# A hybrid attention, recurrence and mixture-of-experts layer: expert weights in 8 KB rows, the overfull path ahead of the first expert pair, and p turned inside the recurrence

## The chip, the core and the metric

One Trainium2 chip, one of its cores. The metric is device time in microseconds of one execution. Kernel before: median 1132.77 us of 3 runs (1131.93 to 1135.42).

## The reference, cut to what matters

One layer over 512 tokens of width 1024, all float32.

```python
h = rmsnorm(x, g_mix)
q, k, v, xr, gr, ga, gb = split(h @ w_in)
A = diff_attention(q, k, v) @ w_attn_br
R = (rg_lru(conv4(xr)) * gelu(gr)) @ w_lru_br
x += (sigmoid(ga) * A + sigmoid(gb) * R) @ w_out
t = rmsnorm(x, g_moe)
# top-1 of 4 groups, top-2 of its 8 experts: 32 experts, FF 512
for e in range(32):
    x += c[e] * ((silu(t @ w_e_gate[e]) * (t @ w_e_up[e])) @ w_e_down[e])
x += sigmoid(rmsnorm(x, g_ple) @ w_ple_gate) * (p @ w_ple_proj)
out = rmsnorm(x, g_final)
```

## The kernel before, in words

Tokens stand in four tiles `t` of 128 rows. Dense weights come as 1 MB pieces `wr`; ScalarE rounds each into `wh` (L157) and VectorE or GpSimd takes the rest `wl` (L160); TensorE then does three matmuls per block (wh with the high and the low half of the input, wl with the high half). `wh` and `wl` have three buffers each.

**The recurrence (to about 193 us).** For each of eight blocks `m` TensorE does xr, the gates, gr and merge (L169 to L171, L354 to L356). `lru_back` runs for two blocks at a time, one pair late: a square root on ScalarE, products on GpSimd (L384), scans `hs` and products on VectorE (L386, L387), `yh` on ScalarE (L389), `yl` on GpSimd. After the last merge TensorE turns `p` (`pT_ps`, eight transposes, L426), ScalarE and VectorE split it in two halves (`pth` L428, `ptl` L429), and 48 matmuls (`pp_ps`, L438 to L440) give p @ w_ple_proj, which goes to DRAM (L443) for the end of the kernel. The R projection follows.

**The experts (598 to 1067 us).** Experts go in 16 pairs. Each takes 12 pieces of 1 MB (gate, up, down, four each; L825), issued by the SyncE queue into a ring of 15 buffers; a piece has 4 KB rows and carries both experts of the pair. `pair_front` (L994) does gate and up, `hidden_t` turns the hidden block (L978), `pair_back` (L1008) does down. `gather` (L700) picks the tokens of two pairs by one-hot matmuls out of `hx`, the normalised rows that `split_tokens` (L683, L684) writes; since a piece holds rows 2p and 2p+1 in partition p, the gather reads `hx` with a stride of 2. `scatter_two` and `comb` (L959 to L970) add the outputs. In `in_order` blocks TensorE keeps the order of the program.

**The overfull path.** An expert has 64 slots. `count` writes `nblk_i`, the number of extra rounds; `tc.If(nb > 0)` (L1135) runs `overflow`, a loop over all experts. It stands between hidden_t of pair 15 and that pair's down block. The data here never take it: `nb` is 0, every engine loads the value and branches past the body.

**The tail (1067 us on).** The weights of the last gate are loaded (`gate_load`, L800), split, and multiplied for four token tiles.

Of the kernel before, what the change touches and what calls it, by code (L numbers as in the profile page):

```python
# [19 lines left out]
P = 128  # L20
D = 1024
# [19 lines left out]
def kernel(  # L41
# [35 lines left out]
    ONCE = 2  # L77

# [36 lines left out]
    gmv = T("gmv")[:4, :256]  # L115
# [98 lines left out]
    nc.sync.dma_start(gmv, g_moe.rearrange("o (h c) -> (o h) c", h=4))  # L214
# [84 lines left out]
    for k in range(2):  # L299
        nc.tensor.transpose(pv[:, 1 + k, 0:4], gmv[:, k:k + 255:2], ident[:4, :4])  # L300
    gm2 = const.tile([P, 8], F32, name="gm2")
    nc.vector.tensor_copy(gm2.rearrange("p (h k) -> p k h", k=2), pv[:, 1:3, 0:4])
# [89 lines left out]

    TB, TA = {}, {}
# [8 lines left out]
    for j in range(4):  # L402
# [19 lines left out]
    pth, ptl = ([lx.tile([P, S], F32R, tag="lx", bufs=4, name=n) for _ in range(2)] for n in ("pth", "ptl"))
    for k in range(2):
        pt = tps("pT_ps")
        for t in range(NT):
            nc.tensor.transpose(pt[:, t, :], pl[t // 2][:, t % 2 * PLE + k * P:t % 2 * PLE + (k + 1) * P], ident)  # L426
        pt = pt.rearrange("p a b -> p (a b)")
        nc.scalar.activation(pth[k], pt, AF.Copy)  # L428
        nc.vector.tensor_sub(ptl[k], pt, f32(pth[k]))  # L429
# [14 lines left out]
    lx_stack.close()  # L444
# [233 lines left out]
    def split_tokens(t, hx):  # L678

        HX[t] = hx  # L680
        for i in range(2):
            cs = slice(i * 512, (i + 1) * 512)
            nc.scalar.activation(hx[:, 0, cs], xm[:, t, cs], AF.Copy, scale=rstd2[:, t:t + 1])  # L683
            nc.vector.scalar_tensor_tensor(hx[:, 1, cs], xm[:, t, cs], rstd2[:, t:t + 1], f32(hx[:, 0, cs]),  # L684
                                           op0=ALU.mult, op1=ALU.subtract)
# [125 lines left out]
    def loads():  # L811
        for pr, nm, src in pair_order():
            for h in range(4):
                n = P if nm == "d" else 2 * P
# [85 lines left out]
    def gather(q):  # L900
# [7 lines left out]
        for k in range(0, KT, 2):  # L908
# [74 lines left out]
    def pair_front(pr, xg, fill):  # L983
# [20 lines left out]
    def pair_back(pr, hT, fill=None):  # L1004
        py = [zps("y_ps") for _ in range(2)]
        for f, i in [(f, i) for f in range(4) for i in range(2)]:
            for e in range(2):
                nc.tensor.matmul(py[i][64 * e:64 * e + 64, :], hT[:, f, 64 * e:64 * e + 64],  # L1008
                                 W[pr, "d", f][0][:, e, i * 512:(i + 1) * 512], start=f == 0, stop=f == 3)
# [5 lines left out]
    def overflow(nb):  # L1015

        scratch = [t.rearrange("p e (k f) -> p (e k) f", k=2) for t in spill]
# [5 lines left out]
        with tc.For_i(0, nb):  # L1023
            with tc.For_i(0, NE) as e:
# [79 lines left out]
    def experts(pr):  # L1104
# [9 lines left out]
        if pr < 15:  # L1114
            expert_outputs(pr)
# [164 lines left out]
```

## Time and profile before

| | |
|---|---|
| median of 3 runs | 1132.77 us |
| the profiled execution, its time | 1134.24 us |
| its span on the core | 1132.5 us |
| TensorE busy | 1090.8 us, 96% |
| VectorE, ScalarE, GpSimd busy | 565.5, 380.4, 155.6 us |
| DMA rate in the expert stage | 409 GB/s |
| mean granted TensorE clock | 0.987 |

Durations below are of the profiled execution; start times are microseconds from the start of its span. "Idle before" names what ended a wait. [...]

### The profile page before, as it was taken

The page shows a single profiled execution, that of the slowest core. Times are in us where ns is not written, and L with a number is a line of the kernel's source. Part 1 is how long each engine was busy: PE and PEld are TensorE (multiplying, and loading weights), DVE is VectorE, ACT ScalarE, POOL GpSimd, SP SyncE. Part 2 cuts the span into 40 slices and gives each one's busy share as a digit, 9 for nine tenths or more (in the row PEclk, how much of TensorE's full clock was granted, in tenths as well). Part 3 has the DMA queues.
Part 4 walks back from the last instruction along what each step waited for, and adds up shares of the span by engine and source line. Part 5 has one row for each costly group of instructions (what it writes and reads, how often), then busy time and mean ns, then how long its engine had stood idle before and what let it go on. Part 6 is the DMA issues. An engine that isn't in the chain of part 4 may idle for free. (4 is left out here: it accounts for less than half of the span.)

```text
span 1132.5 us, 14421 instructions
## 1 busy us (share of the span) xinstructions
PE 1090.8 (96%) x5650; PEld 732.4 (65%) x5650; DVE 565.5 (50%) x1080; ACT 380.4 (34%) x770; POOL 155.6 (14%) x142
## 2 busy tenths in 40 slices
PE   8999996999999999999999999999999999999897
PEld 7777775888788878778984535454535353533376
DVE  6766673325657474764474343433433433232574
ACT  5556554125545463633431202020201111100353
POOL 3242323111212021332100000000000000000021
PEclk9999998999999999999999999999999999999899
DMA  7332143322221312235857999999999999999801
GB/s 207 112 112 75 58 147 110 100 93 75 76 75 38 100 51 75 75 80 203 317 186 259 408 409 408 409 409 409 409 409 409 408 409 409 409 408 407 341 26 56
DMA packets 109794, 259.81 MB, mean 229 GB/s; under 512 B 12477, under 2 KB 56090, under 8 KB 109722
## 3 DMA queue, kind: packets, MB, share of 16 engines
q1 hardware_dynamic: 109722, 258.84, 60.5%
q8 instruction: 46, 0.75, 0.3%
q14 instruction: 26, 0.21, 0.1%
HBM read 254.63 MB, written 4.19 MB: 229 GB/s over the span
## 5 line engine op out<-in xcount | busy, mean ns | idle before, releaser
L157 ACT ACTIVATE wh<-wr 128x1024 fp32r<-128x1024 f32 x81 | 85.6, 1058 | 105.9 <-PE R_ps L170 32.4
L1008 PE MATMUL y_ps<-d,hT 128*64 128x512 f32 x512 | 117.1, 608 | 4.2 <-PEq L1135 3.6
L994 PE MATMUL gu_ps<-g,xg 128*64 128x512 f32 x512 | 116.0, 595 | 0.6 <-DMA g<-in_w_e_gate_dram 0.6
L994 PE MATMUL gu_ps<-u,xg 128*64 128x512 f32 x496 | 110.1, 593 | 1.4 <-DMA u<-in_w_e_up_dram 0.6
L160 DVE TENSOR_TENSOR wl<-wr,wh 128x1024 fp32r<-128x1024 f32 x54 | 73.0, 1352 | 61.5 <-ACT wh L157 60.2
L160 POOL TENSOR_TENSOR wl<-wr,wh 128x1024 fp32r<-128x1024 f32 x27 | 64.9, 2404 | 181.3 <-ACT wh L157 167.8
L999 ACT ACTIVATE sg<-gu_ps 128x512 f32<-128x512 f32 x16 | 9.6, 598 | 232.4 <-PE gu_ps L994 232.4
L1008 PEld LDWEIGHTS y_ps<-d,hT 128*64 128x64 f32 x512 | 35.9, 139 | 74.1 <-issue 68.5
L994 PEld LDWEIGHTS gu_ps<-u,xg 128*64 128x64 f32 x496 | 35.2, 137 | 72.8 <-issue 66.4
L994 PEld LDWEIGHTS gu_ps<-g,xg 128*64 128x64 f32 x512 | 35.2, 137 | 70.8 <-issue 64.6
L1000 DVE TENSOR_TENSOR sg<-sg,gu_ps 128x512 f32<-128x512 f32 x16 | 11.0, 687 | 126.1 <-ACT sg L999 126.1
L202 POOL TENSOR_TENSOR s<-msq,mhalf 128x1 f32<-128x1 f32 x4 | 3.7, 915 | 499.5 <-DVE msq L201 499.5
L971 DVE TENSOR_TENSOR xm<-xm,comb_ps 128x1024 f32<-128x1024 f32 x30 | 36.6, 1221 | 65.5 <-PE comb_ps L970 65.5
L700 PE MATMUL xg_ps<-oneh,wr 128*128 128x256 f32 x384 | 58.3, 291 | 2.1 <-DVE oneh L692 2.1
L953 DVE SCALAR_TENSOR_TENSOR yl<-y_ps,c,yh 128x512 fp32r<-128x512 f32 x30 | 22.5, 750 | 72.9 <-ACT yh L952 71.4
L700 PEld LDWEIGHTS xg_ps<-oneh,wr 128*128 128x128 f32 x384 | 52.7, 201 | 2.7 <-DVE oneh L692 2.2
L952 ACT ACTIVATE yh<-y_ps,c 128x512 fp32r<-128x512 f32 x30 | 20.6, 688 | 100.2 <-PE y_ps L1008 100.2
L171 PE MATMUL merge_ps<-hTh,wl 128*128 128x512 f32 x128 | 51.9, 406 | 0.5 <-POOL wl L160 0.5
L169 PE MATMUL merge_ps<-hTh,wh 128*128 128x512 f32 x128 | 51.5, 402 | 0.0
L170 PE MATMUL merge_ps<-hTl,wh 128*128 128x512 f32 x128 | 51.4, 401 | 0.0
L962 DVE TENSOR_TENSOR xm<-xm,comb_ps 128x512 f32<-128x512 f32 x68 | 43.6, 679 | 2.6 <-PE comb_ps L960 2.6
L921 ACT ACTIVATE xg<-xg_ps,gm 128x256 f32<-128x256 f32 x60 | 25.2, 470 | 49.2 <-PE xg_ps L700 48.8
(328 smaller groups left out, 2512.9 us busy)
## 6 DMA issues: line engine op xcount, KB each, us to landing
g<-in_w_e_gate_dram SPq DMA_DIRECT2D x64, 1024.0 KB, 19.3
d<-in_w_e_down_dram SPq DMA_DIRECT2D x64, 1024.0 KB, 19.8
u<-in_w_e_up_dram SPq DMA_DIRECT2D x62, 1024.0 KB, 20.2
wr<-in_w_in_dram SPq DMA_DIRECT2D x26, 1024.0 KB, 5.1
wr<-in_w_lru_br_dram SPq DMA_DIRECT2D x4, 1024.0 KB
wr<-in_w_attn_br_dram SPq DMA_DIRECT2D x4, 1024.0 KB, 5.3
wr<-in_w_out_dram SPq DMA_DIRECT2D x4, 1024.0 KB, 5.1
wr<-in_w_ple_gate_dram SPq DMA_DIRECT2D x3, 1024.0 KB
```

The source lines that it names most:

```text
L157: nc.scalar.activation(hi, src, AF.Copy)
L160: e.tensor_sub(lo, src, f32(hi))
L169: nc.tensor.matmul(out_ps, wh[:, k, :], th(k), start=k == 0, stop=False)
L170: nc.tensor.matmul(out_ps, wh[:, k, :], tl(k), start=False, stop=False)
L171: last = nc.tensor.matmul(out_ps, wl[:, k, :], th(k), start=False, stop=k == KT - 1)
L700: nc.tensor.matmul(o, HX[t][:, i, c0:c0 + 255:2], oneh[:, t, :], start=t == 0 and i == 0 and k % 2 == 0, stop=t == NT - 1 and i == 1 and k ...
L921: nc.scalar.activation(xg[(k + c) // 2][:, (k + c) % 2, :], pt[:, c, :], AF.Copy, scale=gm2[:, k + c:k + c + 1])
L953: nc.vector.scalar_tensor_tensor(yl, y, c[:, 0:1], f32(yh), op0=ALU.mult, op1=ALU.subtract)
L962: nc.vector.tensor_tensor(xs_, xs_, pc, op=ALU.add)
L971: nc.vector.tensor_tensor(xm[:, t, :], xm[:, t, :], pc.rearrange("p a b -> p (a b)"), op=ALU.add)
L994: last = nc.tensor.matmul(gu[i][64 * e:64 * e + 64, :], xg[k // 2][:, k % 2, o + 64 * e:o + 64 * e + 64], W[pr, nm, k // 2][0][:, e, k % 2 ...
L1008: nc.tensor.matmul(py[i][64 * e:64 * e + 64, :], hT[:, f, 64 * e:64 * e + 64], W[pr, "d", f][0][:, e, i * 512:(i + 1) * 512], start=f == 0 ...
```

## The change

Five parts, on six places of the code (line numbers below are those of before; those of the changed kernel are up to 11 higher, so L157 is L158 there, L994 is L1004, L1135 is L1142).

1. **8 KB pieces.** A piece of weights now holds half of one expert: four rows of gate or up (two of down) per partition, 8 KB in a row. It is still 1 MB. Pieces 0 and 1 of a weight are the first halves of the two experts, so both are needed at the start of a block, and 2 and 3 at its middle.
2. **Rows in the gather's order.** `split_tokens` reads the token row with a stride of four elements and writes it so that the gather reads 128 contiguous columns; `hidden_t` reads with a stride of 2 instead.
3. **The overfull path** moves from the end of the experts to right behind `gather(0)`. It uses the four buffers of pair 0's gate weights as scratch and loads them again.
4. **gate_load(0)** is issued ahead of the last pair's down pieces.
5. **p is turned** in one two-bank PSUM tile ahead of block 7, its halves take a `wh` and a `wl` buffer, and the pp sums of two token tiles share a two-bank tile.

```diff
+    def turn_p():
+        pth = wp.tile([P, 2, S], F32R, tag="wh", bufs=3, name="pth")
+        ptl = wp.tile([P, 2, S], F32R, tag="wl", bufs=3, name="ptl")
+        pt = sps("pT_ps")
+        for k in range(2):
+            for t in range(NT):
+                nc.tensor.transpose(pt[:, k, t * P:(t + 1) * P],
+                                    pl[t // 2][:, t % 2 * PLE + k * P:t % 2 * PLE + (k + 1) * P], ident)
+        nc.scalar.activation(pth, pt, AF.Copy)
+        nc.vector.tensor_sub(ptl, pt, f32(pth))
...
         for m in (2 * j, 2 * j + 1):
+            if m == 7:
+                pth, ptl = turn_p()
             lru_front(m, wx, wg, m % 2)
...
-            pz = zps("pp_ps")
+            if t % 2 == 0:
+                pz2 = sps("pp_ps")
+            pz = pz2[:, t % 2, :]
...
-            nc.scalar.activation(hx[:, 0, cs], xm[:, t, cs], AF.Copy, scale=rstd2[:, t:t + 1])
+            src = xm[:, t, i * 512:(i + 1) * 512].rearrange("q (p k) -> q k p", k=4)
+            hi, lo = (hx[:, n, i * 512:(i + 1) * 512].rearrange("q (k p) -> q k p", k=4) for n in range(2))
+            nc.scalar.activation(hi, src, AF.Copy, scale=rstd2[:, t:t + 1])
...
-                c0 = k // 2 * 256 + k % 2
-                nc.tensor.matmul(o, HX[t][:, i, c0:c0 + 255:2], oneh[:, t, :],
+                nc.tensor.matmul(o, HX[t][:, i, k * P:(k + 1) * P], oneh[:, t, :],
...
+            if pr == 15 and nm == "d":
+                for b in range(W_EARLY):
+                    gate_load(b)
...
-                s_ = src[0, 2 * pr:2 * pr + 2, h * n:(h + 1) * n, :]
+                n, k = (256, 2) if nm == "d" else (512, 4)
+                s_ = src[0, 2 * pr + h % 2, h // 2 * n:(h // 2 + 1) * n, :].rearrange("(p k) f -> p (k f)", k=k)
...
-            nc.tensor.transpose(pt[:, f, :], sg[:, f * P:(f + 1) * P], ident)
+            c0 = f // 2 * 256 + f % 2
+            nc.tensor.transpose(pt[:, f, :], sg[:, c0:c0 + 255:2], ident)
...
+    xg = gather(0)
+    nb = nc.values_load(nblk_i[0:1, 0:1], min_val=0, max_val=4)
+    with tc.If(nb > 0):
+        overflow(nb)
+    load_upto(NRING + ONCE)
     with in_order():
-        xg = gather(0)
-        load_upto(NRING + ONCE)
         SG[0] = pair_front(0, xg, front_fill(0))
         for pr in range(NE // 2):
             experts(pr)
-    spill = [RING("spill") for _ in range(4)]
-    nb = nc.values_load(nblk_i[0:1, 0:1], min_val=0, max_val=4)
-    with tc.If(nb > 0):
-        overflow(nb)
-    with in_order():
-        expert_outputs(15)
```

How the instructions move, at three places. First ScalarE around the merge of block 6 (`mg_1239` before, `mg_1241` now). Before, in the order of the queue (`wh_1242` and `wh_1296` are the xr and gr weights of block 7, `wh_1331` those of merge 7):

```order
L157 ACTIVATE wh_1242<-wr_1098 128x1024 [waits PE_49]
L349 ACTIVATE xch_1138<-xc_1133 128x512 [waits DVE_49]
L157 ACTIVATE wh_1296<-wr_1100 128x1024 [waits PE_49]
L359 ACTIVATE t_r_1149<-gate_ps_1142,hb_297 128x512 [waits PE_49]
L360 ACTIVATE t_i_1150<-gate_ps_1142,hb_297 128x512 [waits Activation_49]
L363 ACTIVATE lru_103<-t_r_1149,hn_301 128x512 [waits Activation_49]
L372 ACTIVATE sq_1187<-gr_ps_1158 128x512
L364 ACTIVATE t_r_1149<-t_r_1149,hn_301 128x512 [waits Activation_49]
L389 ACTIVATE yh_1198<-lru_106 128x512 [waits DVE_49]
L375 ACTIVATE sq_1187<-sq_1187 128x512 [waits DVE_49]
L157 ACTIVATE wh_1331<-wr_1102 128x1024 [waits PE_49,Pool_49]
L389 ACTIVATE yh_1206<-lru_106 128x512 [waits DVE_49]
```

Now (`wh_1257` and `wh_1311` are the xr and gr weights of block 7, `wh_1346` those of merge 7):

```order
L365 ACTIVATE t_r_1151<-t_r_1151,hn_303 128x512 [waits Activation_49]
L390 ACTIVATE yh_1200<-lru_106 128x512 [waits DVE_49]
L376 ACTIVATE sq_1189<-sq_1189 128x512 [waits DVE_49]
L390 ACTIVATE yh_1208<-lru_106 128x512 [waits DVE_49]
L414 ACTIVATE mg_1241<-merge_ps_1212 128x512 [waits PE_49]
L403 ACTIVATE pth_1243<-pT_ps_1245 128x1024 [waits PE_49]
L158 ACTIVATE wh_1257<-wr_1100 128x1024
L158 ACTIVATE wh_1311<-wr_1102 128x1024 [waits Pool_49]
L158 ACTIVATE wh_1346<-wr_1104 128x1024 [waits DVE_49,PE_49]
```

The weights of block 7 were rounded ahead of the second `yh`; now they stand behind it, behind the merge's own activation and behind `pth`.

Second VectorE at the end of the recurrence, with the second half of w_ple_proj (`wl_1444` before, `wl_1440` now). Before:

```order
L160 TENSOR_TENSOR wl_1444<-wr_1397,wh_1443 128x1024 [waits PE_49,Activation_49]
L365 SCALAR_TENSOR_TENSOR lru_104<-t_i_1287,xc_1270 128x512 [waits Activation_49]
L373 TENSOR_SCALAR sq_1324<-sq_1324 128x512 [waits Activation_49]
L374 TENSOR_TENSOR sq_1324<-sq_1324,gr_ps_1295 128x512 [waits DVE_49]
L367 SCALAR_TENSOR_TENSOR lru_105<-lru_105,t_r_1286 128x512 [waits Activation_49,Pool_49]
L376 SCALAR_TENSOR_TENSOR lru_106<-sq_1324,gr_ps_1295 128x512 [waits Activation_49]
L386 SCALAR_TENSOR_TENSOR hs_1363<-lru_103,lru_105 128x512 [waits Pool_49]
L386 SCALAR_TENSOR_TENSOR hs_1371<-lru_103,lru_105 128x512 [waits Pool_49]
L387 SCALAR_TENSOR_TENSOR lru_106<-hs_1363,lru_106 128x512 [waits DVE_49]
L387 SCALAR_TENSOR_TENSOR lru_106<-hs_1371,lru_106 128x512 [waits DVE_49]
L429 TENSOR_TENSOR ptl_1381<-pT_ps_1383,pth_1379 128x512 [waits Activation_49]
```

Now:

```order
L368 SCALAR_TENSOR_TENSOR lru_105<-lru_105,t_r_1301 128x512 [waits Activation_49,Pool_49]
L161 TENSOR_TENSOR wl_1398<-wr_1395,wh_1397 128x1024 [waits DMAHW4_49,PE_49,Activation_49]
L377 SCALAR_TENSOR_TENSOR lru_106<-sq_1339,gr_ps_1310 128x512 [waits Activation_49]
L387 SCALAR_TENSOR_TENSOR hs_1378<-lru_103,lru_105 128x512 [waits DMAHW2_49,Pool_49]
L387 SCALAR_TENSOR_TENSOR hs_1386<-lru_103,lru_105 128x512 [waits DMAHW3_49,Pool_49]
L388 SCALAR_TENSOR_TENSOR lru_106<-hs_1378,lru_106 128x512 [waits DVE_49]
L388 SCALAR_TENSOR_TENSOR lru_106<-hs_1386,lru_106 128x512 [waits DVE_49]
L161 TENSOR_TENSOR wl_1440<-wr_1395,wh_1439 128x1024 [waits PE_49,Activation_49]
```

`ptl` has left this place; the low half of the second weight has come behind the two scans.

Third TensorE where the branch stands. Before, ahead of the last pair's down block:

```order
L978 MATMUL hT_ps<-ident,sg 128x128 [waits DVE_49]
L978 MATMUL hT_ps<-ident,sg 128x128 x3
L1134 TENSOR_LOAD nblk_i [waits DVE_49,PE_49,Pool_49]
L1135 COMPARE_AND_BRANCH
L1023 COMPARE_AND_BRANCH
```

Now, behind the last matmuls of gather(0):

```order
L709 MATMUL xg_ps<-oneh,hx_5229 128x256 [waits Activation_49]
L709 MATMUL xg_ps<-oneh,hx_5229 128x256 x7
L1141 TENSOR_LOAD nblk_i [waits DVE_49,PE_49,Pool_49]
L1142 COMPARE_AND_BRANCH
L1034 COMPARE_AND_BRANCH
```

The load and the branch have moved from the last of the 16 pairs to ahead of the first; what follows the second row in each is the start of the skipped body, and the other four engines' branches move along.

## Rows read from the trace of the kernel before

**Rows 1.** windows: stretch, length, busy by engine, granted clock, DMA share, GB/s.

```profile
650.00:1000.00 350.00, 350.00 (x1774) 165.79 (x1773) 130.83 (x205) 50.73 (x96) 0.00 (x0) 1.00 1.03 409
1000.00:1050.00 50.00, 47.38 (x212) 17.75 (x211) 15.39 (x21) 4.88 (x8) 0.00 (x0) 1.00 1.01 402
```

**Rows 2.** waits of PE, 138 to 195 us: total, times, longest.

```profile
PE pp_ps L440 <- DVE ptl L429: 5.0, 1, 5.0
PE pp_ps L438 <- ACT pth L428: 3.2, 1, 3.2
PE gate_ps L354 <- ACT xch L349: 0.7, 1, 0.7
```

**Rows 3.** windows of the stretches at half the clock; columns as in Rows 1.

```profile
175.30:185.60 10.30, 4.97 (x11) 3.48 (x12) 5.62 (x5) 2.72 (x5) 4.61 (x3) 0.50 0.04 15
588.30:591.80 3.50, 3.48 (x20) 3.38 (x21) 3.19 (x16) 0.21 (x1) 0.00 (x0) 0.51 0.99 401
1052.60:1059.40 6.80, 5.73 (x14) 1.94 (x16) 0.70 (x2) 0.00 (x0) 0.00 (x0) 0.50 0.77 292
```

**Rows 4.** timeline, 149 to 160 us: start, duration, instruction, [idle before <-releaser].

```profile
150.62 0.39 PE L169 MATMUL xr_ps<-hTh,wh 128*128 128x512 f32 x1
...
153.47 2.71 DVE L387 SCALAR_TENSOR_TENSOR lru<-hs,lru 128x512 f32<-128x512 f32 x1
...
156.21 0.64 ACT L389 ACTIVATE yh<-lru 128x512 fp32r<-128x512 f32 x1 [3.08 <-DVE lru L387]
...
157.22 1.05 ACT L157 ACTIVATE wh<-wr 128x1024 fp32r<-128x1024 f32 x1
...
158.30 1.23 DVE L160 TENSOR_TENSOR wl<-wr,wh 128x1024 fp32r<-128x1024 f32 x1 [0.81 <-ACT wh L157]
```

**Rows 5.** timeline, 168 to 190 us, PE and DVE.

```profile
169.83 1.03 PE L426 MATMUL pT_ps<-ident,pl 128*128 128x128 f32 x8
...
172.98 5.48 DVE L386 TENSOR_TENSOR_SCAN hs<-lru 128x512 f32<-128x512 f32 x2 [3.02 <-POOL lru L384]
...
178.39 1.26 DVE L387 SCALAR_TENSOR_TENSOR lru<-hs,lru 128x512 f32<-128x512 f32 x2
```

**Rows 6.** DMA, 620 to 1000 us: queue, packets, MB, share of 16 engines.

```profile
q1 hardware_dynamic: 40229, 155.08, 102.3%
```

**Rows 7.** DMA, 811.5 to 812.0 us: one 8 KB instruction packet in that stretch.

```profile
q14 instruction: 1, 0.01, 3.9%
```

**Rows 8.** timeline of PE, pairs 12 and 13 (first two) and 14 and 15.

```profile
970.49 7.08 PE L994 MATMUL gu_ps<-u,xg 128*64 128x512 f32 x32
...
987.61 7.09 PE L1008 MATMUL y_ps<-d,hT 128*64 128x512 f32 x32
...
1029.92 3.93 PE L994 MATMUL gu_ps<-u,xg 128*64 128x512 f32 x16
...
1037.04 1.94 PE L994 MATMUL gu_ps<-u,xg 128*64 128x512 f32 x8 [0.62 <-SPq L1135]
...
1041.34 5.58 PE L1008 MATMUL y_ps<-d,hT 128*64 128x512 f32 x24
...
1047.55 1.94 PE L1008 MATMUL y_ps<-d,hT 128*64 128x512 f32 x8 [0.62 <-SPq L1135]
```

**Rows 9.** line 1135, and waits of SP, 1000 to 1070 us.

```profile
L1135 PEldq COMPARE_BRANCH  x1: 4932/4932/4932, 1048.3 to 1048.3; - x1
...
SPq L1135 <- SPq L1135: 17.9, 8, 2.9
```

**Rows 10.** timeline, 1046 to 1060 us: ACT, then PE.

```profile
1050.12 0.59 ACT L980 ACTIVATE hT<-hT_ps 128x512 f32<-128x512 f32 x1
...
1053.67 6.47 PE L1008 MATMUL y_ps<-d,hT 128*64 128x512 f32 x16 [3.59 <-PEq L1135]
```

**Rows 11.** timeline, 583 to 599 us: DVE, then PE.

```profile
587.12 0.75 DVE L684 SCALAR_TENSOR_TENSOR hx<-xm,rstd,hx 128x512 fp32r<-128x512 f32 x1 [0.93 <-ACT hx L683]
...
588.32 2.29 PE L700 MATMUL xg_ps<-oneh,wr 128*128 128x256 f32 x9 [2.14 <-DVE oneh L692]
```

More of the change, by code (lines that the diff above doesn't have):

```diff
@@ L77 @@
     ONCE = 2
+    W_EARLY = 1
     def SM(name, shape, dt=F32, bufs=4):
@@ L298 @@
     nc.vector.tensor_copy(colv, pv[:, 0, :NV])
[L299 to L302, printed above, removed]
+    for k in range(4):
+        nc.tensor.transpose(pv[:, 1, 2 * k:2 * k + 2], gmv[:, k:k + 509:4], ident[:2, :2])
+    gm4 = const.tile([P, 8], F32, name="gm4")
+    nc.vector.tensor_copy(gm4.rearrange("p (h k) -> p k h", k=4), pv[:, 1, 0:8].rearrange("p (k h) -> p k h", h=2))
     hb = const.tile([P, 16], F32, name="hb")
@@ L391, in lru_back @@
             Y[m] = (yh, yl)
+    def turn_p():
[8 more added lines that the diff above has]
+        nc.vector.tensor_sub(ptl, pt, f32(pth))
+        return [pth[:, k, :] for k in range(2)], [ptl[:, k, :] for k in range(2)]
     TB, TA = {}, {}
@@ L418 @@
     lru_back((6, 7))
+    lx_stack.close()
     pp_dram = dram.tile([S, D], F32, name="pp_dram")
[L422 to L429, printed above, removed]
     wpp = WR([P, 2, D])
@@ L1008, in pair_back @@
                 nc.tensor.matmul(py[i][64 * e:64 * e + 64, :], hT[:, f, 64 * e:64 * e + 64],
-                                 W[pr, "d", f][0][:, e, i * 512:(i + 1) * 512], start=f == 0, stop=f == 3)
+                                 W[pr, "d", f // 2 * 2 + e][0][:, f % 2 * D + i * 512:f % 2 * D + (i + 1) * 512], start=f == 0, stop=f == 3)
             if fill:
@@ L1015, in overflow @@
     def overflow(nb):
-        scratch = [t.rearrange("p e (k f) -> p (e k) f", k=2) for t in spill]
+        late_routing()
+        scratch = [W[0, "g", h][0].rearrange("p (k f) -> p k f", k=4) for h in range(4)]
         V = lambda n: scratch[n // 4][:, n % 4, :]
@@ L1033, in overflow @@
                 for b in range(2):
+                    px = zps("xs2_ps")
+                    for t in range(NT):
+                        for i in range(2):
+                            nc.tensor.matmul(px, oneh[:, t, :], f32(HX[t][:, i, b * 512:(b + 1) * 512]),
+                                             start=t == 0 and i == 0, stop=t == NT - 1 and i == 1)
+                    nc.scalar.activation(V(13 + b).rearrange("s (p k) -> s k p", k=4), px.rearrange("s (k p) -> s k p", k=4), AF.Copy)
                     pt = tps("xg2_ps")
                     for c in range(4):
+                        nc.tensor.transpose(pt[:, c, :], V(13 + b)[:, c * P:(c + 1) * P], ident)
+                    for c in range(4):
                         k = 4 * b + c
-                        for t in range(NT):
-                            for i in range(2):
-                                nc.tensor.matmul(pt[:, c, :], f32(HX[t][:, i, k * P:(k + 1) * P]), oneh[:, t, :],
-                                                 start=t == 0 and i == 0, stop=t == NT - 1 and i == 1)
                         nc.scalar.activation(xg[b][:, c, :], pt[:, c, :], AF.Identity, scale=colv[:, C_GM + k:C_GM + k + 1])
@@ L1081, in overflow @@
             nc.vector.tensor_scalar(base, base, float(P - 1024 * NE), None, op0=ALU.add)
+        for h in range(4):
+            nc.sync.dma_start(*W[0, "g", h])
     C, SG, HT, PY, YW = {}, {}, {}, {}, {}
@@ L1132 @@
             experts(pr)
-    spill = [RING("spill") for _ in range(4)]
-    nb = nc.values_load(nblk_i[0:1, 0:1], min_val=0, max_val=4)
-    with tc.If(nb > 0):
-        overflow(nb)
-    with in_order():
-        expert_outputs(15)
-    for b in range(4):
+    for b in range(W_EARLY, 4):
         gate_load(b)
```

24 lines of the change are left out of this document (7 added, 17 removed).

## The prediction, made before the changed kernel was run

> **What bounds the kernel now.** Read the busy times first: TensorE is at 96% of the span, no other engine above 50%. So a microsecond counts only if it takes away a wait of TensorE, a stretch at half its clock, or work of its own. The windows by stage say where to look: in the expert stage TensorE is busy 350.00 of 350 us while the DMA engines also stand at 409 GB/s with a share above 1; from 1000 to 1050 us it is down to 47.38 of 50 [rows 1]. The waits of TensorE show two long ones at the end of the recurrence, 3.2 and 5.0 us, and a short one of 0.7 [rows 2]. [...]
>
> The sum is made against the profiled execution, 1134.24 us, which lies 1.5 us above the median of 1132.77. A difference under 0.3% (3.4 us) can't be told from no change.
>
> **p inside the recurrence: a loss of 6.3 us.** Before, the region from the start of block 7 loses 0.7 + 3.2 + 5.0 us in waits, and the slow stretch holds 4.97 us of TensorE work that full clock does in half, 2.5 lost: 11.4 in all [rows 2, 3].
>
> Now TensorE ends merge 6 at 150.7, turns p in 1.03 and is free at 151.7 [rows 4, 5]. Its next matmul needs the rounded xr weights of block 7, which in ScalarE's new order stand behind the second yh, the merge activation and pth. Follow that queue. The second scan ends at 153.47, where its product starts; the product took 2.71 beside a GpSimd split that is no longer there at that time, so I take 0.68, a value between this and half of the pair's 1.26 [rows 4, 5]: 154.15. Then yh 0.64, the merge activation about 0.6 (it runs between the yh and the wh rows, overlapping both a little), pth of 1024 elements 1.05, the wh of the same size 1.05 [rows 4]: 157.4. The low half needs VectorE for ptl (about 1.3) and wl (1.23): 159.0. Four matmuls (0.23 each) need only wh, so the wait is 159.0 - 151.7 - 0.9 = **6.3 us**. With the long product it would be 8.3; below 5 it can't go, since the three operations behind yh take 2.7 and the scan ends at 153.47 in any case.
>
> The second wait: merge 7 used to end at 169.83 and the last product at 179.65, 9.8 later [rows 5]. pp still needs the second half of its weights, and in VectorE's new order wl_1440 stands behind both scans and products. The pair of scans took 5.48 with a GpSimd split beside the second; that split has moved away, so about 1.1 less: wl_1440 is there 9.8 - 1.1 + 1.2 = 9.9 after merge 7. Until then TensorE has 18 matmuls that need only the first half (4.2 us); six of them wait about 1.3 for ScalarE to empty the other bank of their two-bank tile behind the square root and the merge activation. So waits of 1.3 + 4.4, and some 0.5 more for the same kind of tile later. Both long waits are over 2 us, so I price a slow stretch behind each; those in the trace hold 3.5 to 5.7 us of work [rows 3], thus 1.7 to 2.9 lost, and I take 2.6. New loss: 6.3 + 5.7 + 0.5 + 5.2 = 17.7, less 11.4; the transposes themselves are the same eight: **+6.3**. Ends: +1 without slow stretches, +9 with long ones and the long product.
>
> **The end of the experts: a gain of 9.7 us.** Pair 15 waits for weights: its up block takes 9.06 us (1029.92 to 1038.98) against 7.08 two pairs earlier, the down block of 14 takes 8.15 against 7.09 [rows 8]; with the gate block, which has one such wait (0.9, an estimate), 4.0. Then the branch: TensorE's COMPARE_BRANCH took 4.93 us and TensorE idled 3.59 [rows 9, 10]. Without it TensorE still waits for hT, whose activation ends at 1050.71, about 0.75 after its transposes: 2.85 saved. Then the clock: 16 down matmuls took 6.47; at 7.09 for 32 they take 3.55: 2.9 saved [rows 8, 10]. Together 9.7. SyncE's 17.9 us of waiting for its queues in front of the branch [rows 9] goes too; it held back the last two pieces of pair 15, and counts in what follows.
>
> **Does the DMA keep up?** This gain needs earlier pieces. A piece takes 1 MB at 409 GB/s, 2.57 us. Pieces are now needed in twos, so the last of pair 14's down is wanted 1.8 us earlier; gate_load(0) and two pieces stand between it and the start of pair 15's down, 3 x 2.57 = 7.7 after 1047.55, at 1055.2, while TensorE would want them at about 1046.8: 8.4 late. The first buffers also come free 1.8 later (two at once): 10.2 us to make up in the 444 us from 600 to 1044, **2.3%**. The 4 KB packets took 1.023 x 16 x 380 us / 37,861 = 164 ns (155.08 MB) [rows 6]; an 8 KB packet, an instruction fetch, took 0.039 x 16 x 0.5 us = 312 ns in the same stretch, against 328 for two: 5% less [rows 7]. Between nothing and 5% I take 3%, as one row of rounded share is thin, and so the full gain; each per cent below 2.3 costs 4.4 us. [...]
>
> **The branch at its new place: +0.5.** TensorE's sequencer ran ahead of the array (branch at 1048.3, array busy to 1050.1 [rows 9, 10]), so load and branch of half a microsecond hide behind gather(0)'s last 16 matmuls, and the other engines stand idle there. SyncE drains its queues, but has nothing to issue until pair 0 frees a buffer. Above: 4.93 again, 3.6 idle and up to 1.7 of slow clock, +5.3. The skipped body has some 275 TensorE instructions against about 450. [...]
>
> **The row order: +0.3.** The contiguous weight loads save nothing: loads fill 166 of 350 us beside matmuls that never pause [rows 1]. The strided split has passes of 0.75 on VectorE ahead of the one-hot that TensorE waits 2.14 for [rows 11]. If a pass slowed twofold, two would add 1.5; the late routing's small operations leave that chain, perhaps 0.5 less.
>
> Sum: 6.3 - 9.7 + 0.5 + 0.3 = -2.6; 1131.6 in a profile, less 1.5 on the median: **1130.1 us**, too little to tell from no change.
>
> **Rivals.**
> - *The clock holds* through the two new waits of TensorE. p then costs 1.1 (17.7 - 5.2 - 11.4): 1124.9. Against it: every wait of this length in the rows came with a slow stretch. Chance 0.2.
> - *The pieces come no faster* (under 0.9%). Then 6.2 to 10.2 us of lateness move into pair 15, the end gains little or nothing, and p's 6.3 stands uncovered: 1130.1 + 6.2 to 10.2 = 1136.3 to 1140.3, slower. It decides below that 0.9%. For it: only one rounded row speaks against it, and 409 GB/s may be what memory gives. Chance 0.15.
> [...]
> - *The branch misses again* at its new place, now behind gather(0): +4.8, 1134.9. For it: the same instruction took 4.93; against: the shorter body. Chance 0.1.
>
> My forecast has 0.45. It lies 0.7 us short of the bound for faster (1129.4), so of its 0.45 I give 0.18 to faster, 0.25 to no change, 0.02 to slower. The clock rival gives 0.18 faster and 0.02 the same; no faster pieces 0.03 the same and 0.12 slower; the two at 1135 together 0.02 faster, 0.12 the same, 0.06 slower. Faster 0.38, same 0.42, slower 0.20. The range takes in the clock rival with 2.5 us below it and reaches to 1138.5, leaving out about half of the rival above 1136.3: 1122.5 to 1138.5.
>
> **What would show it.** A TensorE wait near 6 us for block 7's xr weights behind pth, at half clock after it; then one near 4.4 for wl_1440. In the experts, no wait for weights in pair 15, a shorter pitch of pieces than 2.57, and pair 15's down 0.75 behind hT at full clock. At 598 us no wait over 1. The forecast is wrong if the clock stays at 1.00 near 155, if pair 15 still waits for pieces, or if TensorE's branch at 598 takes microseconds.

## The result, and the profile after

The changed kernel is **slower**: 1140.75 us (median of 6 runs, 1138.13 to 1141.77) against 1133.01 for the kernel before, a ratio of 1.006 with a 95% interval of 1.0042 to 1.0078. Run once more beside the last experiments it took 1138.01 us, ratio 1.0047 (1.0029 to 1.0065). The prediction said 1130.1, and its range ended at 1138.5. The profiled execution spans 1139.2 us, 6.7 more than the one before, so the two traces can be set against each other stage by stage.

The windows of the changed kernel (stretch, length, busy by engine, granted clock as a share of full speed, DMA share, GB/s), with those of before that were not shown:

```profile
0.00:150.00 150.00, 140.01 (x609) 111.68 (x610) 95.19 (x140) 79.22 (x108) 48.58 (x52) 0.97 0.35 106
650.00:1000.00 350.00, 350.00 (x1778) 166.07 (x1776) 135.93 (x217) 50.70 (x97) 0.00 (x0) 1.00 1.01 419
1000.00:1050.00 50.00, 50.00 (x230) 19.57 (x229) 13.57 (x19) 5.93 (x10) 0.00 (x0) 1.00 1.01 419
```

```profile
0.00:150.00 150.00, 142.00 (x626) 113.10 (x627) 101.14 (x146) 83.44 (x112) 49.53 (x53) 0.99 0.39 120
```

The expert stage did what was forecast: 419 GB/s instead of 409, and TensorE no longer pauses from 1000 to 1050 us [rows 1]. But the first 150 us, which the prediction never spoke of, lost 2 us of TensorE work (140.01 for 142.00) and some clock (0.97 for 0.99). The waits of TensorE over the whole run say where else to look:

```profile
PE xr_ps L170 <- ACT wh L158: 4.6, 1, 4.6
PE gate_ps L355 <- ACT xch L350: 4.5, 3, 3.5
PE pp_ps L449 <- ACT pp L453: 3.9, 3, 2.5
PE gu_ps L1004 <- DVE wts L889: 3.2, 1, 3.2
...
PE ple_ps L1218 <- DVE x2s L1183: 2.4, 1, 2.4
PE xmT_ps L747 <- DVE L L646: 1.8, 2, 1.0
...
PE rk_ps L678 <- DVE ohr L685: 1.2, 1, 1.2
```

Of these the prediction had xr_ps (6.3) and, with other numbers, pp_ps. The 3.5 at the start (1.9 before), the 3.2 at the first expert pair and the 2.4 in the tail are new, and so are the 1.8 and the 1.2 in the routing (none and 0.3 before).

Cutting both traces at TensorE's rows gives the ledger. The stages are: A, to the end of merge 6; B, from there to the end of the R projection (it holds p); C, to the end of the first gather; D, to pair 0's hT transposes; E, to pair 15's hT transposes; F+G, to the last matmul of the final gate (F up to the last expert matmul). Another 7.6 us follow in every run. In us; the labels are those of the experiments below:

| | before | change | e2 | e3 | e5 | e6 | e9 | e10 | e11 |
|---|---|---|---|---|---|---|---|---|---|
| A start | 150.8 | 155.3 | 149.0 | 153.1 | 150.9 | 153.0 | 150.3 | 150.9 | 153.1 |
| B p | 87.4 | 88.7 | 89.0 | 86.9 | 87.3 | 90.0 | 86.9 | 90.0 | 88.9 |
| C attention, routing | 359.7 | 363.4 | 363.0 | 364.0 | 364.0 | 357.8 | 358.9 | 363.9 | 359.8 |
| D first pair | 30.5 | 33.8 | 33.6 | 33.2 | 30.5 | 35.2 | 30.5 | 30.5 | 30.5 |
| E pairs | 421.0 | 416.6 | 416.6 | 416.6 | 416.6 | 418.5 | 418.5 | 416.6 | 422.0 |
| F+G last outputs, tail | 75.5 | 73.8 | 72.2 | 72.2 | 71.5 | 73.8 | 71.7 | 74.0 | 75.8 |

From before to the change: A +4.5, B +1.3, C +3.7, D +3.3, E -4.5, F -4.8, G +3.1; together +6.7. Five of the seven were forecast otherwise: p at +6.3, C and D at +0.8 together, A and G not at all.

### The profile page after: what moved, and what is told of

Same layout as the page of the kernel before. It is cut to its first block, busy times and chain, and to the rows that moved or that the text cites. A ratio compares the mean times of both kernels' runs of the same rounds, so it can differ in the third digit from the quotient of the medians.

```text
span 1139.2 us, 14414 instructions
## 1 busy us (share of the span) xinstructions
PE 1093.4 (96%) x5652; PEld 739.1 (65%) x5652; DVE 566.8 (50%) x1079; ACT 385.8 (34%) x770; POOL 155.5 (14%) x142
## 5 line engine op out<-in xcount | busy, mean ns | idle before, releaser
L158 ACT ACTIVATE wh<-wr 128x1024 fp32r<-128x1024 f32 x81 | 85.5, 1058 | 113.5 <-PE R_ps L171 31.1
L1004 PE MATMUL gu_ps<-g,xg 128*64 128x512 f32 x512 | 115.8, 595 | 3.2 <-DVE wts L889 3.2
L1018 PE MATMUL y_ps<-d,hT 128*64 128x512 f32 x512 | 114.7, 596 | 0.7 <-ACT hT L990 0.7
L1004 PE MATMUL gu_ps<-u,xg 128*64 128x512 f32 x496 | 109.5, 592 | 0.0
L161 DVE TENSOR_TENSOR wl<-wr,wh 128x1024 fp32r<-128x1024 f32 x54 | 72.7, 1347 | 58.5 <-ACT wh L158 57.6
L1004 PEld LDWEIGHTS gu_ps<-g,xg 128*64 128x64 f32 x512 | 37.2, 137 | 71.1 <-issue 66.1
L1004 PEld LDWEIGHTS gu_ps<-u,xg 128*64 128x64 f32 x496 | 35.8, 137 | 70.2 <-issue 69.0
L1206 POOL TENSOR_TENSOR wgl<-wr,wgh 128x1024 fp32r<-128x1024 f32 x2 | 4.7, 2384 | 477.5 <-ACT wgh L1205 477.5
```

The costliest lines, as they stand in the source:

```text
L158: nc.scalar.activation(hi, src, AF.Copy)
L161: e.tensor_sub(lo, src, f32(hi))
```

## Experiments

Ratios are to runs of the kernel before on the same chip. A and B rise and fall by up to 3 us from run to run (A is 155.3 and 152.4 in two profiles of the changed kernel itself, at a mean granted clock of 0.987 and 0.989), so a stage is read where several runs agree. The diff ahead of the prediction leaves out two edits that the runs bear on: the change turns the gain column otherwise (e1, e2), and it shortens the body of the overfull path, which gathers each half of the columns with 8 matmuls and 4 transposes instead of 32 matmuls (e4, e5).

**e1: the gain column's four small transposes, put into the kernel before.** The change reads g_moe in two rows instead of four and turns it by four transposes of 2 rows, not two of 4.

```
...
-    for k in range(2):
-        nc.tensor.transpose(pv[:, 1 + k, 0:4], gmv[:, k:k + 255:2], ident[:4, :4])
+    for k in range(4):
+        c0 = k // 2 * 256 + k % 2
+        nc.tensor.transpose(pv[:, 1, 2 * k:2 * k + 2], gmv[:, c0:c0 + 255:2], ident[:2, :2])
...
```

> The kernel before with one thing of the change: the gain column is turned by four transposes of 2 rows instead of two of 4 rows (same values). Theory: these two more small instructions move the first gate matmuls from behind 15 to behind 9 matmuls of merge 0, TensorE runs dry (3.5 us instead of 1.9) and a stretch of half clock follows near 35 us; block 1 starts at 43.3 us instead of 39.1 and the run takes 1137 us (before: 1133.0). Rival: the late start was x arriving late in that one execution; then block 1 starts at 39.1 to 39.8 and the time is 1133.

1134.57 us, ratio 1.0028 (1.0009 to 1.0046): 1.8 us more than before, between the theory and the rival, and block 1 starts at 40.8.

**e2: the changed kernel with the column loaded by one DMA**, no transposes.

```
...
+    gm4 = const.tile([P, 8], F32, name="gm4")
+    nc.sync.dma_start(gm4.rearrange("p (b k) -> p b k", b=2), g_moe.rearrange("o (b p k) -> p (o b) k", b=2, k=4))
...
-    for k in range(4):
-        nc.tensor.transpose(pv[:, 1, 2 * k:2 * k + 2], gmv[:, k:k + 509:4], ident[:2, :2])
...
```

> The changed kernel, with the gain column brought by one small DMA, without transposes; the first gate stands behind 15 merge matmuls again. Theory: the 4.5 us lost ahead of block 1 come back, block 1 starts near 39.5 us with the granted clock at 1.00 from 15 to 150 us: 1136.4 us (changed kernel: 1140.75). Rival: block 1 late as before, at 43.8, time 1140.7.

1135.33 us, ratio 1.0029 (1.0017 to 1.0040). Against the ratio of the change that is 3.5 us less by its first runs and 2.0 by its second (e12). So two more tiny matmuls cost about 2 us: A is 152.9 on average in the nine profiles that have them (150.9 to 155.3) and 150.6 in the five that don't (149.0 to 153.1). The path is the compiler's static order: before, TensorE did 15 merge matmuls ahead of the first gate matmul; with four transposes it does 9, so it reaches the gate sooner and waits for the same ScalarE result longer. TensorE's waits for it, from 25 or 30 to 45 us, in before, the change, e1 and e2:

```profile
PE gate_ps L354 <- ACT xch L349: 1.9, 1, 1.9
```

```profile
PE gate_ps L355 <- ACT xch L350: 3.5, 1, 3.5
```

```profile
PE gate_ps L355 <- ACT xch L350: 2.5, 1, 2.5
```

```profile
PE gate_ps L351 <- ACT xch L346: 0.7, 1, 0.7
```

In the change's wait of 3.5 us (32.7 to 36.2) the granted clock falls to 0.50, from 35.2 to 42.0. The windows of five half-clock stretches of the changed kernel, the first of them this one (5.78 us of work, so 2.9 lost); both kernels have one more near 11 us (from 11.5 to 14.9 before, from 11.3 to 14.7 in the change) and one at the very end (from 1127.7 and from 1134.3 on):

```profile
35.20:42.00 6.80, 5.78 (x14) 4.52 (x15) 3.64 (x8) 2.16 (x4) 0.00 (x0) 0.50 0.62 202
161.50:164.90 3.40, 3.19 (x9) 2.50 (x9) 1.80 (x2) 0.17 (x1) 0.00 (x0) 0.50 0.46 114
188.80:192.20 3.40, 3.15 (x7) 2.37 (x8) 0.78 (x1) 1.20 (x3) 3.15 (x2) 0.50 0.58 155
598.40:601.80 3.40, 3.40 (x22) 3.31 (x21) 3.02 (x13) 0.00 (x0) 0.00 (x0) 0.50 1.01 424
1079.70:1083.10 3.40, 3.40 (x10) 2.63 (x9) 3.40 (x7) 2.46 (x5) 0.88 (x1) 0.50 0.00 0
```

In these runs it is a matter of odds: with 9 merge matmuls ahead, seven of nine profiles show a half-clock stretch near 35 us; with 15, one of five (e11). The wait of 3.2 us at the first expert pair, at 610 us, is followed by none (granted clock 1.00 from 610.6 to 617.4).

**e3: the changed kernel with p turned where it was before.** The edit is the change's part on `turn_p` and `pz2`, undone.

> The changed kernel with p turned and split behind the recurrence as it was. Theory (from the two traces): p's part costs 1.3 us in the changed kernel, so 1139.5 us; from the end of merge 6 to the first R matmul 42.6 us as before instead of 43.9. Rival (the step of the prediction): it costs 6.3, so 1134.4 us.

1136.75 us, ratio 1.0036 (1.0023 to 1.0050), between theory and rival; against the 1138.0 of e12 it is the theory's 1.3. B falls from 88.7 to 86.9.

**e11: the kernel before with p alone turned as in the change.**

> The kernel before with p alone turned as in the change (early, two banks, ScalarE's and VectorE's passes of 1024 elements, two-bank projections). Theory A: it costs what the changed kernel's profile shows for it, 1.3 to 1.8 us: about 1134.5 us. Rival B, the prediction's term: 6.3 us, about 1139.3 us. Rival C: nothing, because the shorter recurrence (scans waiting 3.4 us instead of 5.5) pays for the wait at the turn: 1133 us.

1135.09 us, ratio 1.0022 (1.0012 to 1.0032), 1.6 us above before; B +1.5. So p costs 1.3 to 1.8, theory A, and not 6.3. The waits in e11 from 138 to 195 us are the long ones of the changed kernel to the digit:

```profile
PE xr_ps L169 <- ACT wh L157: 4.6, 1, 4.6
PE pp_ps L448 <- ACT pp L452: 3.9, 3, 2.5
```

**e4: the changed kernel with the rows in natural order**, the gather reading its stationary with a stride of four columns; the overfull path's body is then the longer one of the kernel before.

```
-                nc.tensor.matmul(o, HX[t][:, i, k * P:(k + 1) * P], oneh[:, t, :],
+                c0 = k // 4 * 512 + k % 4
+                nc.tensor.matmul(o, HX[t][:, i, c0:c0 + 509:4], oneh[:, t, :],
```

> The changed kernel with the normalised rows stored in natural order: the split passes read and write without a stride, and the gather and the overfull path read every fourth column instead. Theory: the strided split (1.24 us on ScalarE and 1.13 on VectorE instead of 0.73 and 0.75) costs 3.7 us between the last out projections and the gather; undone, 1137.0 us. Rival: the time lies in the gather's strided weight loads; then the gather's 64 matmuls take longer than 7.8 us per pair of pairs and the time stays at 1140 or rises by up to 8 x 0.5 us.

1189.35 us, ratio 1.0493 (1.0464 to 1.0522): the rival's cause, at over ten times its price. E is 51.7 longer than in the change, 7.4 for each of its seven gathers. The loads of the gather, 625 to 1000 us, grouped by line, in e4, the change (stride 1) and before (stride 2):

```profile
L710 PEld LDWEIGHTS xg_ps<-oneh,wr 128*128 128x128 f32 x288 | 71.7, 330 | 0.2
```

```profile
L709 PE MATMUL xg_ps<-oneh,wr 128*128 128x256 f32 x336 | 48.2, 279 | 0.0
L709 PEld LDWEIGHTS xg_ps<-oneh,wr 128*128 128x128 f32 x336 | 43.8, 188 | 0.5
```

```profile
L700 PE MATMUL xg_ps<-oneh,wr 128*128 128x256 f32 x336 | 49.7, 285 | 0.0
L700 PEld LDWEIGHTS xg_ps<-oneh,wr 128*128 128x128 f32 x336 | 45.2, 196 | 0.5
```

In e4 the 288 loads fill 71.7 of TensorE's 74.6 us: the load sets the pace of the gather and is no longer hidden. In the kernel before it nearly did so already, with 45.2 of 49.7 us; the average over the stage, loads of 166 in 350 us [rows 1], hid that. So some reordering in `split_tokens` is needed for 8 KB rows; the question is which.

**e6: pairs of columns kept together.** The same number of passes and elements, but each reads runs of two elements; the gather has stride 2 again.

```
-            src = xm[:, t, i * 512:(i + 1) * 512].rearrange("q (p k) -> q k p", k=4)
+            src = xm[:, t, :].rearrange("q (p a c) -> q a p c", a=2, c=2)[:, a]
...
-                nc.tensor.matmul(o, HX[t][:, i, k * P:(k + 1) * P], oneh[:, t, :],
+                c0 = k // 2 * 256 + k % 2
+                nc.tensor.matmul(o, HX[t][:, i, c0:c0 + 255:2], oneh[:, t, :],
```

> The changed kernel with the normalised rows in another order: two neighbours stay together, so that the split passes read runs of two elements (8 bytes) at a stride of 16 bytes, and the gather's stationary reads every second column, as in the kernel before. As many instructions and elements as in the changed kernel. Theory A: the passes are slow (1.24 us on ScalarE, 1.13 on VectorE, against 0.73 and 0.75) because they read single elements 16 bytes apart, and that is what made the stretch of the output projection and routing 3.7 us longer: with runs of two about half comes back, passes of 0.9 to 1.0 us and a time of about 1138.5 us (1137 if runs of two cost nothing). Rival B: the price is of the access pattern having one more dimension, whatever its stride: passes stay at 1.1 to 1.25 us and the time at 1140.8 us. Rival C: the passes get faster but were hidden, and the 3.7 us came from the clock: passes under 1.0 us and 1140.8 us all the same.

1136.58 us, ratio 1.0032 (1.0015 to 1.0049). The split's passes, 420 to 600 us, in the change and in e6:

```profile
L694 ACT ACTIVATE wr<-xm,rstd 128x512 fp32r<-128x512 f32 x6 | 7.1, 1220 | 3.0 <-PE out_ps L731 2.3 <-POOL rstd L203 0.7
L695 DVE SCALAR_TENSOR_TENSOR wr<-xm,rstd,wr 128x512 fp32r<-128x512 f32 x6 | 6.8, 1136 | 2.2 <-ACT wr L694 2.2
```

```profile
L694 ACT ACTIVATE wr<-xm,rstd 128x512 fp32r<-128x512 f32 x6 | 4.4, 768 | 3.0 <-PE out_ps L732 2.3 <-POOL rstd L203 0.7
L695 DVE SCALAR_TENSOR_TENSOR wr<-xm,rstd,wr 128x512 fp32r<-128x512 f32 x6 | 4.3, 752 | 0.8 <-ACT wr L694 0.7
```

Runs of two give back nearly all, more than theory A hoped. C falls by 5.6, of which 1.7 only moves into D (the half-clock stretch of 3.4 us lies at 604.8 there, behind the gather's end); E rises by 1.9, as the 448 matmuls of seven gathers are some 4 ns slower each (284 ns for 279 to 280). The single-element stride thus cost about 3.9, and the contiguous gather paid 1.9 of it back.

**e7: the first gather's evacuations ahead of the branch** on ScalarE and VectorE.

```
...
-    nb = nc.values_load(nblk_i[0:1, 0:1], min_val=0, max_val=4)
+    with tc.issue_after(evac['s'].ins), tc.issue_after(evac['v'].ins):
+        nb = nc.values_load(nblk_i[0:1, 0:1], min_val=0, max_val=4)
```

> The changed kernel with one thing moved: ScalarE and VectorE carry out the first gather's last evacuations ahead of the branch, not behind it. Theory A: the 3.16 us that TensorE waits ahead of the first expert matmul are the evacuations standing behind the branch, with the activation table that ScalarE loads again after it (1.28 us): the gap falls to under 1 us, about 1138.3 us. Rival B: the branch itself (register load on every engine, compare, jump) takes the time: TensorE's gap stays at 2.5 to 3.2 us, 1140.8 us. Rival C: the gap goes, but ScalarE's table load and the late loads come back as a wait in the first pair: 1140 us.

1136.46 us, ratio 1.0036 (1.0022 to 1.0051). The gap fell from 3.16 to 2.18, not below 1: between the theories. In the changed kernel all four evacuations of ScalarE stand behind the branch, and two of VectorE's four, and ScalarE loads a table of its activation functions again:

```profile
607.48 1.28 ACT L930 ACT_TABLE_LOAD   x1 [10.01 <-PE xg_ps L709]
...
608.78 0.84 ACT L930 ACTIVATE xg<-xg_ps,gm 128x256 f32<-128x256 f32 x2
...
610.58 0.74 PE L1004 MATMUL gu_ps<-g,xg 128*64 128x512 f32 x2 [3.16 <-DVE wts L889]
```

In e7 the same evacuations run first, and TensorE starts when ScalarE has passed the branch behind them:

```profile
607.49 1.77 ACT L931 ACTIVATE xg<-xg_ps,gm 128x256 f32<-128x256 f32 x4 [10.55 <-PE xg_ps L709]
...
609.59 1.93 PE L1005 MATMUL gu_ps<-g,xg 128*64 128x512 f32 x7 [2.18 <-ACTq L1144]
```

But the evacuations alone don't set the gap. In e3, where the branch stands as in the change, TensorE starts while ScalarE still evacuates:

```profile
606.31 0.84 ACT L921 ACTIVATE xg<-xg_ps,gm 128x256 f32<-128x256 f32 x2
...
606.58 0.74 PE L995 MATMUL gu_ps<-g,xg 128*64 128x512 f32 x2 [2.56 <-DVE gs L877]
```

What all eight profiles with the path at the start share is SyncE, the engine that issues the weight loads. It jumps past the body like the others, then waits on eight semaphores one after another, and the first expert matmul starts among those eight: at 603.87 (603.5 to 604.0) in e2, 606.58 (606.2 to 606.7) in e3, 609.59 (609.1 to 609.6) in e7. In the change SyncE's branch stands at 606.4. Here are its eight waits behind it, then TensorE's wait in e2, which the trace puts down to SyncE:

```profile
L1142 SPq EVENT_SEMAPHORE  x8: 17/17/17, 610.2 to 610.7; - x8
```

```profile
PE gu_ps L1000 <- SPq L1138: 3.0, 1, 3.0
```

From SyncE's branch to the first of the eight 2.7 to 3.7 us pass; what it does in that time the traces don't show. No run took SyncE's branch and waits away, so how much of the gap would be left to ScalarE (its first two evacuations in the change end at 609.62) is open.

At its new place the branch stands where the engines come to it together: in the change all five take it between 606.1 and 607.3, in the kernel before between 596.5 (GpSimd) and 1051.3 (VectorE). What stands behind it there starts late: SyncE's waits at 610.2, ScalarE's evacuations at 608.78 and 609.71, TensorE's first expert matmul at 610.58.

**e5: the overfull path back at the end**, with the change's shorter body and early gate load.

```
...
     count()
-    xg = gather(0)
+    with in_order():
+        xg = gather(0)
+        load_upto(NRING + ONCE)
+        SG[0] = pair_front(0, xg, front_fill(0))
+        for pr in range(NE // 2):
+            experts(pr)
+    spill = [RING("spill") for _ in range(4)]
     nb = nc.values_load(nblk_i[0:1, 0:1], min_val=0, max_val=4)
     with tc.If(nb > 0):
         overflow(nb)
-    load_upto(NRING + ONCE)
     with in_order():
-        SG[0] = pair_front(0, xg, front_fill(0))
-        for pr in range(NE // 2):
-            experts(pr)
+        expert_outputs(15)
```

> The changed kernel with the overfull path where it was before, behind pair 15's first half (its shorter body kept, its scratch in four ring buffers again). Theory A: the 3.2 us between the first gather and the first expert matmul (gather end 607.42, first gu matmul 610.58) belong to the branch standing there: without it that gap is under 0.5 us. At the end the branch comes back; if its price there is the fetch of code behind a long body, it is about 4.9 us again on TensorE's queue and the half clock behind it, so about 1140.8 - 2.8 + 4.9 = 1142.9 us. Theory B: the shorter body takes the price at the end too (0.4 us as at the start): about 1138.5 us. Rival C: the gap at the start is the weights' or the gather's and stays: about 1145.5 us. The first weights of the first gate matrix are loaded earlier here, which should change nothing.

1132.65 us, ratio 0.9996 (0.998 to 1.0012): below every theory, though theory B has the branch right. D is back at 30.5. And F+G is not longer than with the path at the start but shorter: 71.5 against 73.8. TensorE's branch instruction by line, in before, in e5 (at the end) and in the change (at the start):

```profile
L1135 PEldq COMPARE_BRANCH  x1: 4932/4932/4932, 1048.3 to 1048.3; - x1
```

```profile
L1149 PEldq COMPARE_BRANCH  x1: 358/358/358, 1046.4 to 1046.4; - x1
```

```profile
L1142 PEldq COMPARE_BRANCH  x1: 352/352/352, 606.2 to 606.2; - x1
```

All three profiles with the old body at the end (before, e1, e11) have 4.75 to 4.93 us here; all ten with the new one have 0.35 to 0.36, at either place. And e4, which has the longer body at the start:

```profile
L1139 PEldq COMPARE_BRANCH  x1: 3652/3652/3652, 604.2 to 604.2; - x1
```

What made TensorE's own branch dear in these runs was not where it stood but what it jumped over (e4 differs from the change in the rows and in that body alone).

**e10: e5 with the first gate matrix loaded behind the last pair**, `W_EARLY = 0`.

> e5 (the overfull path at the end) with the load of the first gate matrix back behind the last pair, as in the kernel before. Theory A: the tail of e5 was 3 to 5 us shorter (last expert matmul to last gate matmul 54.50 us, against 57.62 before and 59.1 to 60.8 in the changed kernel) because the splits of that matrix run on VectorE while TensorE is held at the branch: without the early load TensorE waits for the splits again, the step is 57.6 us and the time about 1135.7 us. Rival B: the branch's pause alone gives VectorE its lead, whatever is loaded: the step stays 54.5 to 55 us and the time 1132.7 us.

1135.7 us, ratio 1.0025 (1.0016 to 1.0034): theory A's time to the tenth, in part by luck. The step from the last expert matmul to the last gate matmul is 59.6, not 57.6, and the outputs ahead of it are 2.6 shorter than in e5 (14.4 against 17.0); together, F+G is 74.0 against 71.5. TensorE's waits in the last outputs and the tail, in e10 and in e5:

```profile
PE y_ps L1018 <- DVEq L1149: 2.0, 1, 2.0
PE ple_ps L1221 <- DVE wgl L1214: 2.0, 1, 2.0
```

```profile
PE y_ps L1018 <- DVEq L1149: 2.0, 1, 2.0
```

In e5 TensorE does not wait for `ple_ps` there. So the branch at the end still costs TensorE a wait of 2.0, but the tail of e5 finds the first gate matrix split. That is done among the last outputs, from 1061.84, and not, as theory A had it, while TensorE is held at the branch (until 1051.98). The changed kernel splits this matrix as early:

```profile
1060.23 2.48 DVE L1210 SCALAR_TENSOR_TENSOR wgl<-wr,colv,wgh 128x1024 fp32r<-128x1024 f32 x2
```

What its tail has in TensorE's way is VectorE's first pass over the third gate matrix, which stands ahead of the `x2s` that TensorE waits 2.4 for:

```profile
1075.15 3.23 DVE L1206 TENSOR_TENSOR wgl<-wr,wgh 128x1024 fp32r<-128x1024 f32 x1
1078.31 0.41 DVE L1183 TENSOR_TENSOR x2s<-x2T_ps,x2s 128x256 fp32r<-128x256 f32 x1
```

That pass took 3.23 us beside a GpSimd split (two passes from 1072.59 to 1077.30), against 1.21 for the same ones at 1078.96, 1080.61 and 1082.27, behind that split. TensorE's 2.4 and the half-clock stretch at 1079.7 follow. In e5 the pass stands behind `x2s`:

```profile
1069.47 0.42 DVE L1187 TENSOR_TENSOR x2s<-x2T_ps,x2s 128x256 fp32r<-128x256 f32 x1 [0.48 <-ACT x2s L1186]
...
1071.97 1.80 DVE L1210 TENSOR_TENSOR wgl<-wr,wgh 128x1024 fp32r<-128x1024 f32 x1 [0.60 <-ACT wgh L1209]
```

No run changed this order alone.

**e8: a first combination**, the path still at the start: gain column by DMA, p undone, `W_EARLY = 0`, evacuations first.

> The changed kernel with what the runs so far point to: the gain column by one DMA (no small transposes ahead of the first gate), p turned where it was before, all gate weights loaded where they were before, and the evacuations ahead of the branch. Kept of the change: the 8 KB pieces, the row order, the overfull path behind the first gather. Theory A: the parts add: 1140.8 - 5.4 (gain column) - 1.8 (p) - 2.5 (evacuations) - 1.5 (gate weights) = 1129.6 us, 3.4 under the kernel before. Rival B: TensorE's clock and the waits take back what one part gives, as the first run of the gain column showed less in the profile than in the time: 1133 us, no difference from the kernel before.

1133.49 us, ratio 1.0007 (0.9996 to 1.0018): rival B's time. Against the change's profile A fell by 5.2 and F+G by 1.5, as theory A had it, but D by 0.6 only (33.2) and B by 0.9. The single-element split (C 363.0), the branch behind the first gather and the late gate matrix were all still in it.

**e9: the combination that the other runs point to.** e5 with e6's rows, e2's gain column and e3's p.

> What the runs so far point to: of the change, the 8 KB pieces, the shorter overfull path, and the first gate matrix's early load are kept; the overfull path stands at the end again (as in e5), the rows keep pairs of columns together (as in e6), the gain column comes by one DMA (as in e2), p is turned where it was before (as in e3). Theory A: the parts add. From e5's 1132.65 us: rows in pairs -5.6 in the routing and +3.3 in the seven gathers (stride 2 again), so -2.3; p -1.5; the order of TensorE at the start -2 to -3: 1126 to 1127 us, 6 us (0.5%) under the kernel before. Rival B: TensorE's clock or a later wait takes back what each gives, as in e8: 1131 to 1133 us.

**1127.35 us, ratio 0.9954 (0.9939 to 0.9969)**: theory A within a microsecond, and 6 us under the kernel before. By stages, against e5, the rows gave what was priced and more (C -5.1, E +1.9), the start and p less (A -0.6, B -0.4). Its expert stage has the DMA rate of the change (420 GB/s from 650 to 1000 us), with TensorE busy 350.00 of 350 us.

**e12: the change once more**, as a base on that chip.

> The changed kernel itself, beside the others on this chip, as the base that the differences are taken from. First measured at 1140.75 us (6 runs). The runs with one part taken away were 1135.3 (gain column), 1136.8 (p), 1136.6 (rows in pairs), 1136.5 us (evacuations first), each about 4 us lower, while their profiles show 1 to 6 us: theory A, the change's time is 1139 to 1141 us and these differences hold; rival B, the six runs lay high, and it is about 1138 us.

1138.01 us: rival B. Its stages are those of the first profile within 0.2 us, but for A, which is 2.9 shorter. The parts taken out singly (e2, e3, e6, e7: 1.3 to 2.7 us below these 1138.0) are therefore read with the 2 to 3 us by which A wanders; the stages carry the verdicts.

## Why the prediction was wrong

1. **The DMA keeps up: right.** 419 GB/s against 409 is 2.4%, just above the 2.3% that was needed and below the 3% taken from one packet. Of the two at 1135 whose chances are given together, one stands for a rate about 1% higher, the author's estimate; no run shows that term, the runs showed 2.4%.
2. **The end of the experts, -9.7: right up to the last expert matmul, then a third given back.** E and F fell by 9.3. Of this the late weights are about 2.5 (forecast 4.0) and the branch 2.8 (2.85): TensorE starts pair 15's down block 1.43 after hT instead of 4.25. The half clock is 2.0 (2.9): the block with its scatters takes 11.62 instead of 13.63. And 1.9 came from the contiguous gather, which the prediction had put at nothing because weight loads are hidden on the stage's average: 336 matmuls of the gather kept TensorE busy for 48.2 us instead of 49.7. The step that failed is the silent one, that time gained ahead of the tail reaches the end. G rose by 3.1: VectorE's queue now has a pass of 3.23 over the third gate matrix ahead of what TensorE waits for, and a stretch at half clock follows. e5 shows that the move itself was worth nothing at this end. The dear branch was gone with the shorter body alone.
3. **"The branch at its new place, +0.5": wrong, +3.3.** The rival that it misses again did not happen (352 ns). That a shorter body would make it cheap was the author's estimate; e5, with that body at the old place, shows it (358 ns against 4932). The step asked only what TensorE's own branch costs. It said that "the other engines stand idle there", but six of the gather's eight evacuations stood behind the branch, with a table load of 1.28 ahead of ScalarE's. And it said that SyncE "drains its queues, but has nothing to issue", while TensorE's first expert matmul starts only among SyncE's eight waits in all eight profiles, the first of them 2.7 to 3.7 us behind SyncE's branch. The prediction read the 17.9 us of these waits [rows 9] as standing in front of the branch. In the kernel before they stand behind SyncE's, which is at 1034.7, and two waits of TensorE in [rows 8] are put down to SyncE at that line:

```profile
L1135 SPq EVENT_SEMAPHORE  x8: 17/17/17, 1035.2 to 1052.6; - x8
```

4. **"The row order, +0.3": mis-sized.** The passes slowed by 1.5 to 1.7 times, inside the twofold bound that was named, yet C lost 3.7. The prediction counted two of VectorE's eight passes, the ones ahead of the last one-hot; the others delay VectorE's routing, for which TensorE now waits (xmT_ps 1.8, rk_ps 1.2; in e6, none and 0.3). Net of the faster gathers the part costs about 2.
5. **p, +6.3: mis-sized, +1.3 to +1.8.** The order of the queues came as written. The first wait was 4.6 instead of 6.3: it ended with the rounded high half of the weights (`wh`), and TensorE did not wait for the low half, which the prediction had at its end. Then came three waits for ScalarE's evacuations, 3.9 together, and none on wl_1440, which had been put at 4.4. The half-clock stretches held 3.19 and 3.15 us of work and lost 1.6 each, not 2.6. Each lies at a wait over 2 us (4.6 and 2.5), as priced; the 3.2 us at 610 have none.
6. **A, the start, was not in the sum.** The reason was there to be read: the order of TensorE's instructions moved at a place whose own edit looked harmless. Over all runs this is worth about 2 us, not the 4.5 of one profile.

The errors partly cancelled: p was too dear by 5, and what was missed came to about 14 (A 4.5, C 3.4, D 2.8, G 3.1), or 11 with the A of e12. So the forecast of a small gain had its largest gain right and none of its rivals was one of these four losses.

In the traces a packet of 16 KB of instructions starts inside the dear branch of TensorE (at 1050.77 in that of 1048.32 to 1053.25 in the kernel before, at 605.15 in that of 604.18 to 607.83 in e4), and behind the cheap one of the change (at 607.24, the branch ends at 606.52). That the branch's time is spent on this fetch was not shown beyond that. No run varied the body's length alone, in steps, so from what length on the branch is dear was not shown either.

## What to carry to other kernels

Read the new static order of every engine wherever the diff touches an instruction, not only where it means to move one: here two tiny transposes cost about as much as the whole of p (about 2 us against 1.3 to 1.8). Price a branch by what every engine has ahead of it and behind it, SyncE's waits for its queues included, and by the length of what it skips (4.75 to 4.93 us on TensorE's queue with the long body at the end, 0.35 to 0.36 with the short one), before moving it. Of a gain on TensorE ahead of a tail, count only as much as the other engines' work in the tail is ready earlier too: of the 9.3 us gained in E and F, 3.1 went again in G.

## What the runs showed of the hardware

- A stationary load of the gather, 128 columns of 4 bytes, took 330 ns at a stride of 16 bytes (e4), 196 at a stride of 8 (before) and 188 without one (the change). On ScalarE and VectorE single elements 16 bytes apart took 1220 and 1136 ns where runs of two took 768 and 752.
- ScalarE loaded an activation table again (1.28 us) behind the branch in all eight profiles with the path at the start, though the body did not run; in none of the six with the path at the end.
- SyncE's first wait came 2.7 to 3.7 us behind its branch with the path at the start; with the path at the end 0.5 in before, e1 and e11, 2.1 in e5, e9 and e10.
- The half-clock stretches inside these fourteen profiles lasted 3.4, 6.8 or 10.2 us, at what looks like the same place with one length in one run and another in the next (35 us: 6.8 in the change, 3.4 when it ran again).
